# S5 rotation levels in wide operations, whole-table loads, an earlier SSD step-size stage and a split group norm, in a hybrid decoder trunk on one core

## The chip, the cores and the metric

One core of one Trainium2 chip runs the whole program. The core has a matrix engine (TensorE, "PE" in the profile; its weight loads are listed apart as "PEld"), three elementwise engines (VectorE "DVE", ScalarE "ACT", GpSimd "POOL") and a queue of DMA issues on SyncE ("SP"). Each engine takes its instructions in the order in which they stand on it, and semaphores make one engine wait for another. The metric is the time of the program on the device in microseconds; lower is better.

## The reference

Two decoder layers over 512 positions of width 1024, in float32. Layer 0 runs two sequence mixers side by side from one input projection, gates them, and projects back. Layer 1 is a multi-scale retention layer. Only layer 0 is touched here. Cut to what matters:

```python
def s5_mixer(u, ...):                  # 64 groups of 16 channels, 64 complex states each
    ab = exp(lr*dt) * (cos(li*dt) + 1j*sin(li*dt))      # one step of the state's decay and turn
    # x[t] = ab * x[t-1] + bb @ u[t]   (associative scan in chunks), y = Re(c @ x)
    y = gelu(y + d_skip*u)
    return y * sigmoid(y @ glu_w + glu_b)

def ssd_mixer(xbc, dt_raw, ...):       # 16 heads of 64, state 128
    xbc = silu(causal_depthwise_conv(xbc, conv_w, conv_b))
    dt = softplus(dt_raw + dt_bias)
    # chunked scan with decay exp(cumsum(-dt * exp(a_log)))

def rmsnorm(x, w, n_groups):           # SSD output times silu(z): two groups of 512 channels
    return x * rsqrt(mean(x*x, per group) + eps) * w
```

## The kernel before

Activations lie transposed: 128 channels on the partitions, 512 positions along the row, eight such tiles for the model width. A projection onto 128 output channels is a `proj`: in plain float32 (`mm1`, 8 matmuls of 512 columns), or for the names in `SPLIT` with weights and inputs split into a high and a low fp32r part (`mm3`, 24 matmuls). The accumulators of the projections (`acc`) are three PSUM tiles used in turn.

Layer 0 first normalises its input: squares on ACT, added on DVE, summed over the partitions on PE against a column of ones (`rs0ps`), inverse root on DVE (`rs0ms` to `rs0y`), spread over the partitions by transposes (`rs0pb`) and copied to `rbc`; `xn` is the product. Three S5 input projections, u0 to u2, run on the input that is not normalised yet, between the loads.

After that, layer 0 is a list of stages, `ORDER`. Each word is a letter and a number: x are the SSD input projections with their conv (DVE, three `scalar_tensor_tensor` on the PSUM tile), d the SSD step sizes (`steps`), e the decays (`decay`), u the S5 inputs, z the gates, q the S5 parameters, l and g the loading of an S5 block's input and tables, a its scan, k and b its taps, c its output, w the split of `xn`, s and t the SSD chunks, n and r the SSD norm, p the S5 gate, o the SSD half of the output projection. The list sets the priority; a scheduler then places each engine's instructions, so that the work of neighbouring stages is interleaved on an engine. The order on each engine is fixed when the program is built.

**The S5 rotation.** The scan needs a table `rot` with the turn of every state at every block of eight steps, 64 blocks for 32 columns of states. It is built by doubling, on POOL (`cmul`): from n blocks to 2n by a complex product with the turn at n blocks, the level `lv`. The levels come from DVE: `square()` squares a complex number of 32 columns and pulls its length back to one, ten small operations; it runs three times ahead of the first level and once between levels, and two copies write each level into `lvs`. All six levels cost 94 small DVE instructions.

**The tables.** `al_d` is a table in DRAM that the stage g reads back into `al` for each half block, `al[16 * tt:16 * tt + 16]` at a time, so that eight DMAs of 64 KB fill one `al`. The S5 input is written to `u_d` and read back to `U` in eight DMAs as well. The operators `T` of the taps are loaded in the same eight-piece manner.

**The products O.** Stage b forms the S5 output operators on POOL, `O<-ct,s5pws`, from a loaded table `ct`, eight products and four sums for each block.

**The SSD norm.** `ssd_norm` (stage n) loads a gate, applies it on POOL, squares on ACT into the gate's tile `zb`, and adds the squares of a group's four tiles on POOL. `ssd_parts` (stage r) calls `rstd`: four matmuls against ones (`rsg0ps`), the inverse root on DVE, the spread by transposes (`rsg0pb`), and then the products and splits into `ybh` and `ybl` that the output projection `ob` reads.

## Time and profile before

| | |
|---|---|
| time, median of 3 runs | 933.45 us (933.06 to 939.46) |
| the profiled execution, its own time | 927.74 us |
| its span in the profile | 925.9 us |
| busy: PE, DVE, ACT, POOL | 876.2, 553.2, 357.8, 226.2 us |
| instructions on PE, DVE, ACT, POOL | 4252, 986, 569, 193 |

The profiled execution took 927.74 us, of which the span covers 925.9; 1.8 us lie outside it. It was 5.7 us quicker than the median. Times in the profile are counted from the start of the span. Layer 0 takes its first 400 us and a little more.

### The profile page before, as it was taken

What the parts mean: (1) busy time and instruction counts of PE and PEld (TensorE: products, weight loads), DVE (VectorE), ACT (ScalarE), POOL (GpSimd) and SP (SyncE); (2) the same over time, 40 slices, a digit from 0 to 9 for tenths busy, and PEclk for the clock granted to TensorE, in tenths of its full rate; (3) what the DMA queues carried; (4) which work ended last, traced back from release to release, by engine and by line L of the source; (5) the groups of instructions that cost most, each with busy time, mean ns of one, the idle gap of its engine ahead of it and who ended that gap; (6) DMA issues with size and microseconds to landing.
All of it is one profiled execution on the core that took longest, in us unless ns stands there. A gap on an engine that the chain in (4) does not pass through costs nothing.

```text
span 925.9 us, 11510 instructions
## 1 busy us (share of the span) xinstructions
PE 876.2 (95%) x4252; PEld 670.6 (72%) x4252; DVE 553.2 (60%) x986; ACT 357.8 (39%) x569; POOL 226.2 (24%) x193
## 2 busy tenths in 40 slices
PE   8888898998989978999999999999999999999996
PEld 4323346776757766888888888888888888888885
DVE  7999847785893385733454464744643544547445
ACT  4312283252514453623433335345421243254442
POOL 0399445025380930000003121301000203110020
PEclk9998999997998988999999999999999999999999
...
GB/s 241 171 201 140 67 134 91 166 164 226 203 37 275 244 196 137 228 239 125 184 142 129 91 92 69 69 92 67 92 92 91 92 92 69 91 69 69 114 69 91
DMA packets 73623, 121.44 MB, mean 131 GB/s; under 512 B 27552, under 2 KB 38112, under 8 KB 73440
## 3 DMA queue, kind: packets, MB, share of 16 engines
...
q8 instruction: 33, 0.54, 0.2%
...
HBM read 103.61 MB, written 17.07 MB: 130 GB/s over the span
## 4 chain that ended last, share of the span: by engine, by line
PE 76%; DVE 7%; DMA 6%; ACT 4%; issue 3%; SPq 2%; POOL 2%; ACTq 0%; POOLq 0%
PE xbc L205 7%; PE g L115 3%; PE qk L117 3%; PE g L116 3%; PE qk L116 3%; PE g L117 3%; PE qk L115 3%; PE v L930 3%; PE v L931 3%; PE v L929 3%; PE z L117 2%; PE z L115 2%; PE z L116 2%; PE gl L115 2%; PE gl L116 2%
## 5 line engine op out<-in xcount | busy, mean ns | idle before, releaser
L903 POOL TENSOR_TENSOR rt<-rt,ru 128x512 f32<-128x512 f32 x16 | 27.2, 1721 | 134.7 <-DVE ru L902 134.7
L972 POOL TENSOR_TENSOR os<-os,os 128x512 f32<-128x512 f32 x12 | 15.5, 1292 | 139.8 <-ACT os L970 106.9
L798 POOL TENSOR_TENSOR O<-ct,s5pws 128x512 f32<-128x512 f32 x16 | 22.7, 1421 | 81.5 <-DMA ct<-in_s5c_dram 73.4
L882 POOL TENSOR_TENSOR hs<-hs,hs 128x512 f32<-128x512 f32 x7 | 12.3, 1757 | 92.4 <-ACT hs L880 92.4
L347 DVE SCALAR_TENSOR_TENSOR cva<-xbc,cvw,cva 128x511 f32<-128x511 f32 (+2 forms) x36 | 26.7, 741 | 12.3 <-ACT cva L344 11.9
L902 DVE TENSOR_TENSOR ru<-qk,tab 128x512 f32<-128x512 f32 x16 | 11.0, 686 | 32.4 <-PE qk L117 32.4
L392 ACT ACTIVATE dec<-dec,nacs 128x128 f32<-128x128 f32 x64 | 19.4, 389 | 16.6 <-DMA dec<-at_d 16.6
L349 ACT ACTIVATE cva<-cva 128x512 f32<-128x512 f32 x12 | 7.6, 630 | 41.3 <-DVE cva L347 41.2
L798 POOL TENSOR_TENSOR ot<-ct,s5pws 128x512 f32<-128x512 f32 x16 | 21.8, 1364 | 0.0
L802 POOL TENSOR_TENSOR O<-O,ot 128x512 f32<-128x512 f32 x16 | 21.6, 1379 | 0.0
L447 POOL TENSOR_TENSOR za6r<-za6r,y 128x512 f32<-128x512 f32 x1 | 2.0, 2044 | 79.2 <-ACT ob6h L107 79.2
L844 PE MATMUL Y<-Or,X 128*64 128x128 f32 x64 | 13.6, 297 | 8.1 <-DMA Or<-o_d 8.1
L1004 DVE TENSOR_TENSOR h<-h,out 128x512 f32<-128x512 f32 x8 | 5.5, 687 | 25.5 <-PE out L117 25.5
L1065 POOL TENSOR_TENSOR fin<-fin,fnw 128x512 f32<-128x512 f32 x4 | 5.0, 1294 | 58.5 <-ACT fq L1029 58.5
L516 DVE TENSOR_TENSOR h<-oa,h 128x512 f32<-128x512 f32 x8 | 5.5, 691 | 19.6 <-PE oa L117 19.6
L845 PE MATMUL Y<-T,U 128*64 128x128 f32 x128 | 16.7, 290 | 0.0
L411 PE MATMUL y<-ident,yos 128*128 128x128 f32 x48 | 12.7, 351 | 4.0 <-DVE yos L387 4.0
L487 DVE TENSOR_TENSOR hb<-ob,hb 128x512 f32<-128x512 f32 x8 | 5.5, 690 | 17.8 <-PE ob L117 17.8
L205 PE MATMUL xbc<-xn,xbc11w 128*128 128x512 f32 x16 | 9.2, 727 | 6.9 <-issue 6.9
L120 ACT ACTIVATE rh<-rt 128x512 fp32r<-128x512 f32 (+1 forms) x16 | 9.1, 577 | 16.9 <-POOL rt L903 16.9
L121 DVE TENSOR_TENSOR rl<-rt,rh 128x512 fp32r<-128x512 f32 (+1 forms) x16 | 14.9, 957 | 0.6 <-ACT rh L120 0.2
L411 PEld LDWEIGHTS y<-ident,yos 128*128 128x128 f32 x48 | 8.1, 209 | 9.2 <-issue 4.5
...
## 6 DMA issues: line engine op xcount, KB each, us to landing
al<-al_d SPq DMA_DIRECT2D x64, 64.0 KB, 3.3
...
b<-in_s5bP_dram SPq DMA_DIRECT2D x8, 512.0 KB, 4.5
dec<-at_d SPq DMA_DIRECT2D x8, 512.0 KB, 5.6
T<-kd SPq DMA_DIRECT2D x64, 64.0 KB, 2.7
...
```

What stands on the lines that cost most here:

```text
L115: pe.matmul(ps, wh[:, k, :], xh[k], start=start and i == 0, stop=False)
L116: pe.matmul(ps, wh[:, k, :], xl[k], start=False, stop=False)
L117: pe.matmul(ps, wl[:, k, :], xh[k], start=False, stop=stop and i == len(ks) - 1)
L205: pe.matmul(ps, raw[:, k, :], x[k], start=k == 0, stop=k == KD - 1)
L347: vec.scalar_tensor_tensor(g[:, d:], ps[:, 0:SEQ - d], cvw[:, m, j:j + 1], g[:, d:], op0=ALU.mult, op1=ALU.add)
L411: pe.matmul(ps_y[:, pr * P:(pr + 1) * P], yo[:, pr * P:(pr + 1) * P], ident, start=True, stop=False)
L798: pool.tensor_tensor(x.rearrange("p (g k c) -> p g k c", g=4, c=16), ct[:, c, par, 4 * hf:4 * hf + 4].unsqueeze(2).broadcast_to(sh), pws[: ...
L802: pool.tensor_tensor(o, o, tm, op=ALU.add)
L903: pool.tensor_tensor(t1, t1, t2, op=op)
L929: pe.matmul(ps[c], hh[kk][:, cs], wh[:, i, :], start=kk == 0, stop=False)
L930: pe.matmul(ps[c], hh[kk][:, cs], wl[:, i, :], start=False, stop=False)
L931: pe.matmul(ps[c], hl[kk][:, cs], wh[:, i, :], start=False, stop=kk == KD - 1)
```

## The change

The six levels of the rotation are no longer got by squaring one from the other. The angle of one block, `th`, is multiplied by 8, 16, ... 256 in six small operations into one tile of 192 columns, reduced to a turn, and put through the sine and cosine polynomial that the S5 parameters already use, now a function `sin_cos`. All levels are then there at once, after 25 DVE instructions of 192 or 384 columns in place of 94 of 32.

`al_d` has another layout, written by sixteen DMAs of eight partitions each, before two of 64; a whole `al` is then read by one DMA, and a whole `U` too. `T` keeps its eight pieces with another order of partitions.

In `ORDER` the step sizes d0 come first and the decays e0 right after x9. The input projection u2 leaves the head of the program (as 8 float32 matmuls) and stands beside u3 (as 24 split ones). r1 moves ahead of z10.

In the SSD norm the POOL additions go. PE sums the four square tiles of a group itself, sixteen matmuls against ones for each group in place of four; they and the inverse root (`root`) now belong to stage n, and the spread (`spread`) stays in stage r.

On DVE, just after the first normalisation, before. The names `s5scr` are the operands of `square()`; `cva` is a conv:

```order
L661 TENSOR_TENSOR s5scr_433<-s5scr_433 128x32
L662 TENSOR_TENSOR s5scr_433<-s5scr_433 128x32
L663 TENSOR_TENSOR s5scr_433<-s5scr_433 128x32
L347 SCALAR_TENSOR_TENSOR cva_268<-xbc_257,cvw,cva_268 128x511
L664 TENSOR_SCALAR s5scr_433<-s5scr_433 128x32
L347 SCALAR_TENSOR_TENSOR cva_268<-xbc_257,cvw,cva_268 128x510
L665 TENSOR_TENSOR s5scr_433<-s5scr_433 128x32
L666 TENSOR_TENSOR s5scr_433<-s5scr_433 128x32
L347 SCALAR_TENSOR_TENSOR cva_268<-xbc_257,cvw,cva_268 128x509
L675 COPY s5lv<-s5scr_433 128x32
L676 COPY s5lv<-s5scr_433 128x32
```

and after, at the place where the levels now begin; `s5al` is the table for `al_d`:

```order
L661 TENSOR_SCALAR s5lv_506<-s5scr_368 128x32 x6
L528 TENSOR_TENSOR s5cm_445<-s5pw,s5scr_436 128x8x32
L529 TENSOR_TENSOR s5cm_446<-s5pw,s5scr_436 128x8x32
L662 TENSOR_SCALAR s5lv_507<-s5lv_506 128x192
L530 TENSOR_TENSOR s5al<-s5cm_445,s5cm_446 128x8x32
L663 TENSOR_SCALAR s5lv_507<-s5lv_507 128x192
L665 SCALAR_TENSOR_TENSOR s5lv_506<-s5lv_507,s5lv_506 128x192 x3
L562 TENSOR_SCALAR s5lv_508<-s5lv_506 128x192
L563 SCALAR_TENSOR_TENSOR s5lv_507<-s5lv_508 128x192
L564 TENSOR_SCALAR s5lv_508<-s5lv_507 128x192
L352 SCALAR_TENSOR_TENSOR cva_293<-xbc_282,cvw,cva_293 128x511
```

The chain of small squarings that ran between the convs for all six levels has become one block of wider operations, which ends among the convs of xbc8 and xbc10; behind it no squaring stands on DVE.

On POOL, before, the end of the rotation and what follows it (`O` and `ot` are the second block's output operators):

```order
L522 TENSOR_TENSOR s5rt<-rot,s5lv 128x512
L523 TENSOR_TENSOR s5rt<-rot,s5lv 128x512
L524 TENSOR_TENSOR rot<-s5rt 128x32x16
L525 TENSOR_TENSOR s5rt<-rot,s5lv 128x512
L526 TENSOR_TENSOR s5rt<-rot,s5lv 128x512
L527 TENSOR_TENSOR rot<-s5rt 128x32x16
L798 TENSOR_TENSOR O_882<-ct_880,s5pws 128x512
L798 TENSOR_TENSOR ot_883<-ct_880,s5pws 128x512
L798 TENSOR_TENSOR O_888<-ct_880,s5pws 128x512
```

and after:

```order
L789 TENSOR_TENSOR O_808<-ct_794,s5pws 128x512
L789 TENSOR_TENSOR ot_809<-ct_794,s5pws 128x512
L789 TENSOR_TENSOR O_814<-ct_794,s5pws 128x512
L789 TENSOR_TENSOR ot_815<-ct_794,s5pws 128x512
L528 TENSOR_TENSOR s5rt<-rot,s5lv 128x512
L529 TENSOR_TENSOR s5rt<-rot,s5lv 128x512
L793 TENSOR_TENSOR O_796<-O_796,ot_797 128x512
L793 TENSOR_TENSOR O_802<-O_802,ot_803 128x512
L793 TENSOR_TENSOR O_808<-O_808,ot_809 128x512
L793 TENSOR_TENSOR O_814<-O_814,ot_815 128x512
L530 TENSOR_TENSOR rot<-s5rt 128x32x16
L733 TENSOR_TENSOR tm_958<-al_956,b_957 128x512 x2
```

The second block's products and sums stood behind the whole rotation; now they stand inside its last doubling, ahead of the last operation that completes `rot`.

On PE around the SSD norm, before; `K` are the S5 taps, `zb0r` and `zb4r` the tiles of squares, `ob` the output projection:

```order
L814 MATMUL K_2583<-O_1955,s5bd_651 32x128
L166 MATMUL rsg0ps<-ones,zb0r 128x1 x4
L172 MATMUL rsg0pb<-ident,rsg0y 128x128 x4
L166 MATMUL rsg1ps<-ones,zb4r 128x1 x4
L115 MATMUL ob_2889<-ybh_2636,ob0h 128x512
L115 MATMUL ob_2941<-ybh_2636,ob1h 128x512
L116 MATMUL ob_2889<-ybl_2637,ob0h 128x512
L117 MATMUL ob_2889<-ybh_2636,ob0l 128x512
L115 MATMUL ob_2889<-ybh_2641,ob0h 128x512
```

and after; z is the gate projection z9, `S` the scan input of the fourth S5 block:

```order
L115 MATMUL z_2581<-xh_913,z9h 128x512
L116 MATMUL z_2581<-xl_914,z9h 128x512
L166 MATMUL rsg0ps<-ones,zb0r 128x1
L166 MATMUL rsg0ps<-ones,zb1r 128x1
L746 MATMUL S_2268<-U_2121,tm_2125 64x64 x8
L166 MATMUL rsg0ps<-ones,zb2r 128x1
L746 MATMUL S_2268<-U_2121,tm_2136 64x64 x8
L117 MATMUL z_2581<-xh_913,z9l 128x512
```

The sum over the squares stood behind the taps and ahead of the output projection, one matmul for each 128 positions. Now it stands in the middle of the gate projection z9, one matmul for each of the four tiles (and each 128 positions), and each waits for its own tile.

```diff
@@ -26,15 +26,15 @@
 WARM = 11
-SPLIT = [f"z{m}" for m in range(16)] + [f"u{m}" for m in range(3, 8)]
+SPLIT = [f"z{m}" for m in range(16)] + [f"u{m}" for m in range(2, 8)]
 SILU_Z = tuple(range(8, 16))
 GELU_P = ()
 AX, AZ = 200, 600
 KEEP = (2, 3)
 POOL_Z = (7,)
 VEC_X = ((0, 0), (1, 0), (0, 1), (1, 1))
-ORDER = """x8 x10 d0 x9 x11 q0 x0 b0 x1 x2 l0 g0 x3 e0 x4 k0 x5 b1 x6 a0 x7 w0 g1 s0 u3 l1 t0 s1 z0 a1 k1 b2 z1 t1 s2 u4 c0 u5
- t2 l2 g2 s3 z2 a2 k2 b3 z3 t3 u6 c1 u7 z4 l3 g3 z5 n0 z6 a3 z7 c2 n1 z8 k3 r0 z9 z10 r1 c3 z11 o0 p0 p1 o1 z12 p2 z13 p3 o2 z14
+ORDER = """d0 x8 x10 x9 e0 x11 q0 x0 b0 x1 x2 l0 g0 x3 x4 k0 x5 b1 x6 a0 x7 w0 g1 s0 u2 u3 l1 t0 s1 z0 a1 k1 b2 z1 t1 s2 u4 c0 u5
+ t2 l2 g2 s3 z2 a2 k2 b3 z3 t3 u6 c1 u7 z4 l3 g3 z5 n0 z6 a3 z7 c2 n1 z8 k3 r0 z9 r1 z10 c3 z11 o0 p0 p1 o1 z12 p2 z13 p3 o2 z14
@@ -159,7 +159,7 @@
 
-    def rstd(sqs, n, name, bc):
+    def root(sqs, n, name):
@@ -167,10 +167,17 @@
         rsqrt_small(y, ps[:, 0:4], n, name)
+        return y
+
+    def spread(y, name, bc):
         pb = aux(name + "pb")
         for c in range(NC4):
             pe.transpose(pb[:, c * P:(c + 1) * P], y[:, c:c + 1].broadcast_to([P, P]), ident)
         act.activation(bc, pb, AF.Copy)
+
+    def rstd(sqs, n, name, bc):
+        y = root(sqs, n, name)
+        spread(y, name, bc)
...
@@ -235,12 +242,11 @@
                 sq.append(q)
-            pu = [acc(f"u{m}") if m < 2 else aux(f"u{m}", "b") for m in range(3)]
+            pu = [acc(f"u{m}") for m in range(2)]
             for k in range(KD):
                 pe.matmul(pu[0], w0[0][:, k, :], xs[k], start=k == 0, stop=k == KD - 1)
             rstd(sq[:1], D, "rs0", rbc)
             mm1(pu[1], w0[1], xs)
-            mm1(pu[2], w0[2], xs)
...
@@ -257,22 +263,21 @@
         def s5_in(m):
-            ps = proj(a["w_u"][m], f"u{m}") if m > 2 else pu[m]
+            ps = proj(a["w_u"][m], f"u{m}") if m > 1 else pu[m]
             with rank_e():
                 us = t("p", f"us{m}")
                 ud, sd = us.rearrange("p (t k) -> p t k", t=T5), ps.rearrange("p (k t) -> p t k", t=T5)
-                if m > 2:
+                if m > 1:
                     act.activation(ud, sd, AF.Copy)
                 else:
                     vec.tensor_tensor(ud, sd, rbc.rearrange("p (k t) -> p t k", t=T5), op=ALU.mult)
-                sp.dma_start(u_d[:, m * P:(m + 1) * P, :].rearrange("t c k -> c t k"),
-                             us.rearrange("p (t k) -> p t k", t=T5))
+                sp.dma_start(u_d[m * P:(m + 1) * P, :], us[:, 0:SEQ])
 
         def s5_begin(_):
             s5.update(s5_params(s5pr))
             s5_setup(s5)
 
-        for m in range(3):
+        for m in range(2):
@@ -459,15 +464,13 @@
                 act.activation(zt, yb[m], AF.Square)
-                if i:
-                    pool.tensor_tensor(sqs[0], sqs[0], zt, op=ALU.add)
                 sqs.append(zt)
-            held["sq", gr] = sqs
+            held["root", gr] = root(sqs, 512, f"rsg{gr}")
 
         def ssd_parts(gr):
-            yb, sqs = xbc[0:8], held["sq", gr]
+            yb = xbc[0:8]
             rg = t("m", f"rg{gr}")
-            rstd(sqs[:1], 512, f"rsg{gr}", rg)
+            spread(held["root", gr], f"rsg{gr}", rg)
@@ -555,6 +558,17 @@
 
+        def sin_cos(hh, qq, zz, th, n):
+            vec.tensor_scalar(hh[:, 0], th, 0.5, None, op0=ALU.mult)
+            vec.scalar_tensor_tensor(n, hh[:, 0], -1.0, hh[:, 0], op0=ALU.mult, op1=ALU.max)
+            vec.tensor_scalar(hh[:, 1], n, -1.0, 0.5 * math.pi, op0=ALU.mult, op1=ALU.add)
+            vec.tensor_tensor(zz, hh, hh, op=ALU.mult)
+            vec.tensor_scalar(qq, zz, 1.0 / math.factorial(13), None, op0=ALU.mult)
+            for k in (11, 9, 7, 5, 3):
+                sg = 1.0 if (k // 2) % 2 == 0 else -1.0
+                vec.scalar_tensor_tensor(qq, qq, sg / math.factorial(k), zz, op0=ALU.add, op1=ALU.mult)
+            vec.scalar_tensor_tensor(qq, qq, 1.0, hh, op0=ALU.add, op1=ALU.mult)
+
@@ -575,19 +589,9 @@
             vec.scalar_tensor_tensor(th, n, -cst, th, op0=ALU.mult, op1=ALU.add)
-        hh = scr2[:, 0]
-        vec.tensor_scalar(hh[:, 0:W], th, 0.5, None, op0=ALU.mult)
-        vec.scalar_tensor_tensor(n, hh[:, 0:W], -1.0, hh[:, 0:W], op0=ALU.mult, op1=ALU.max)
-        vec.tensor_scalar(hh[:, W:], n, -1.0, 0.5 * math.pi, op0=ALU.mult, op1=ALU.add)
-        zz = scr2[:, 1]
-        vec.tensor_tensor(zz, hh, hh, op=ALU.mult)
-        qq = scr2[:, 2]
-        vec.tensor_scalar(qq, zz, 1.0 / math.factorial(13), None, op0=ALU.mult)
-        for k in (11, 9, 7, 5, 3):
-            sg = 1.0 if (k // 2) % 2 == 0 else -1.0
-            vec.scalar_tensor_tensor(qq, qq, sg / math.factorial(k), zz, op0=ALU.add, op1=ALU.mult)
-        vec.scalar_tensor_tensor(qq, qq, 1.0, hh, op0=ALU.add, op1=ALU.mult)
-        sh, ch = qq[:, 0:W], qq[:, W:]
+        hh, zz, qq = (scr2[:, i].rearrange("p (i w) -> p i w", w=W) for i in range(3))
+        sin_cos(hh, qq, zz, th, n)
+        sh, ch = qq[:, 0], qq[:, 1]
@@ -636,10 +640,11 @@
                 act.activation(pws[64:128, par, 1:8, c], pw[q, 0:7, c, 0:32], AF.Copy, scale=1.0 - 2.0 * c)
-        al_d = dp.tile([8, 2, 64, 2, 32], F32, name="al_d")
-        for h in range(2):
-            sp.dma_start(al_d[:, :, :, h].rearrange("k c x f -> x (k c) f"),
-                         al[64 * h:64 * h + 64].rearrange("p k c f -> p (k c) f"))
+        al_d = dp.tile([8, T5, 2, 8, 2, 32], F32, name="al_d")
+        for jp in range(8):
+            for h in range(2):
+                sp.dma_start(al_d[jp, :, :, :, h].rearrange("k c x f -> x (k c) f"),
+                             al[64 * h + 8 * jp:64 * h + 8 * jp + 8].rearrange("p k c f -> p (k c) f"))
@@ -647,33 +652,26 @@
         pool.memset(rot[:, 1, :, 0:1], 0.0)
-        h32 = [P, 32]
-        scr4 = scr4[:, 0:192].rearrange("p (i w) -> p i w", w=32)
-        ca, sa, cb_, sb_, w1, w2 = (scr4[:, i] for i in range(6))
-        vec.tensor_scalar(ca, cm_[:, 0:32], 1.0, None, op0=ALU.add)
-        vec.tensor_copy(sa, st[:, 0:32])
-
-        def square():
-            vec.tensor_tensor(w1, ca, ca, op=ALU.mult)
-            vec.tensor_tensor(w2, sa, sa, op=ALU.mult)
-            vec.scalar_tensor_tensor(sb_, ca, 2.0, sa, op0=ALU.mult, op1=ALU.mult)
-            vec.tensor_tensor(cb_, w1, w2, op=ALU.subtract)
-            vec.tensor_tensor(w1, cb_, cb_, op=ALU.mult)
-            vec.tensor_tensor(w2, sb_, sb_, op=ALU.mult)
-            vec.tensor_tensor(w1, w1, w2, op=ALU.add)
-            vec.tensor_scalar(w1, w1, -0.5, 1.5, op0=ALU.mult, op1=ALU.add)
-            vec.tensor_tensor(ca, cb_, w1, op=ALU.mult)
-            vec.tensor_tensor(sa, sb_, w1, op=ALU.mult)
-
-        for _ in range(3):
-            square()
+        lvs = t("m", "s5lv", n=384).rearrange("p (n i w) -> p n i w", i=2, w=32)
+        NL = 6
+        sl = [P, NL, 32]
+        ang, cnt_, sc, q2 = (f(f"s5lv{i}", [P, 2, NL, 32]) for i in range(4))
+        th_, n_ = ang[:, 0], cnt_[:, 0]
+        for i in range(NL):
+            vec.tensor_scalar(th_[:, i], th[:, 0:32], 8.0 * 2 ** i, None, op0=ALU.mult)
+        vec.tensor_scalar(n_, th_, 0.5 / math.pi, MAGIC, op0=ALU.mult, op1=ALU.add)
+        vec.tensor_scalar(n_, n_, MAGIC, None, op0=ALU.subtract)
+        for cst in (TWO_PI_1, TWO_PI_2, TWO_PI_3):
+            vec.scalar_tensor_tensor(th_, n_, -cst, th_, op0=ALU.mult, op1=ALU.add)
+        sin_cos(sc, q2, cnt_, th_, n_)
+        sh, ch = q2[:, 0], q2[:, 1]
+        vec.scalar_tensor_tensor(lvs[:, :, 1], sh, 2.0, ch, op0=ALU.mult, op1=ALU.mult)
+        vec.scalar_tensor_tensor(n_, sh, -2.0, sh, op0=ALU.mult, op1=ALU.mult)
+        vec.tensor_scalar(lvs[:, :, 0], n_, 1.0, None, op0=ALU.add)
         n = 1
         rt = f("s5rt", [P, 2, 32, 16])
-        lvs = t("m", "s5lv", n=384).rearrange("p (n i w) -> p n i w", i=2, w=32)
         while n < NK:
             lv = lvs[:, n.bit_length() - 1]
-            vec.tensor_copy(lv[:, 0], ca)
-            vec.tensor_copy(lv[:, 1], sa)
@@ -682,8 +680,6 @@
             n *= 2
-            if n < NK:
-                square()
@@ -722,20 +718,15 @@
         U = f(f"U{j}", [P, 16, NK])
-        for tt in range(T5):
-            sp.dma_start(U[16 * tt:16 * tt + 16],
-                         u_d[tt, 256 * j:256 * j + 256, :].rearrange("(g c) k -> c g k", c=16))
+        sp.dma_start(U, u_d[256 * j:256 * j + 256, :].rearrange("(g c) (t k) -> (c t) g k", c=16, k=NK))
         s5["U"][j] = U
 
     def s5_state(s5, j):
         s5["P"][j] = []
         for par in range(2):
-            g0 = 16 * j + 8 * par
             al, b, tm = (f(f"{n}{j}{par}", [P, 2, 8, 2, 32]) for n in ("al", "b", "tm"))
-            for tt in range(T5):
-                src = s5["al_d"][T5 - 1 - tt, :, g0:g0 + 8].rearrange("c g h f -> c (g h f)")
-                sp.dma_start(al[16 * tt:16 * tt + 16].rearrange("p c g h f -> p c (g h f)"),
-                             src.partition_broadcast(16))
+            src = s5["al_d"][2 * j + par].rearrange("k c g h f -> k (c g h f)")[::-1]
+            sp.dma_start(al.rearrange("p c g h f -> p (c g h f)"), src.unsqueeze(0).broadcast_to([16, T5, 1024]))
...
```

## Rows read from the trace of the kernel before

**Rows 1.** The page: busy time, share and instructions by engine.
```profile
PE 876.2 (95%) x4252; PEld 670.6 (72%) x4252; DVE 553.2 (60%) x986; ACT 357.8 (39%) x569; POOL 226.2 (24%) x193
```

**Rows 2.** Windows: busy time (instructions) of PE, PEld, DVE, ACT, POOL; PEclk, DMA.
```profile
60.00:80.00 20.00, 13.11 (x29) 5.44 (x28) 19.59 (x42) 3.05 (x4) 19.01 (x28) 0.83 0.57 163
...
400.00:925.00 525.00, 517.41 (x2419) 433.16 (x2417) 263.55 (x427) 196.69 (x294) 62.05 (x40) 1.00 0.30 100
```

**Rows 3.** PE, in order of time; start, duration, [idle before <-releaser].
```profile
24.41 0.95 PE L166 MATMUL rs0ps<-ones,xq 128*128 128x1 f32 x8
...
35.37 8.82 PE L205 MATMUL xbc<-xn,xbc8w 128*128 128x512 f32 x16 [1.62 <-DVE xn L245]
44.02 7.03 PE L205 MATMUL xbc<-xn,xbc10w 128*128 128x512 f32 x16
...
71.98 3.75 PE L205 MATMUL xbc<-xn,xbc11w 128*128 128x512 f32 x4 [6.89 <-issue]
...
99.52 8.80 PE L205 MATMUL xbc<-xn,xbc2w 128*128 128x512 f32 x16 [4.12 <-issue]
```

**Rows 4.** DVE, groups in the first 125 us, mean ns of one.
```profile
L663 DVE TENSOR_TENSOR s5scr<-s5scr 128x32 f32<-128x32 f32 x8 | 4.1, 509 | 0.1
...
L675 DVE COPY s5lv<-s5scr 128x32 f32<-128x32 f32 x6 | 1.8, 295 | 0.0
```

**Rows 5.** DVE, in order of time, around the first normalisation.
```profile
25.39 0.16 DVE L150 TENSOR_SCALAR rs0ms<-rs0ps 128x4 f32<-128x4 f32 x1
...
32.81 0.17 DVE L159 SCALAR_TENSOR_TENSOR rs0y<-rs0t,rs0y 128x4 f32<-128x4 f32 x1
...
33.91 0.19 DVE L661 TENSOR_TENSOR s5scr<-s5scr 128x32 f32<-128x32 f32 x1
...
34.63 5.14 DVE L245 TENSOR_TENSOR xn<-x,rbc 128x512 f32<-128x512 f32 x8
...
47.55 1.14 DVE L661 TENSOR_TENSOR s5scr<-s5scr 128x32 f32<-128x32 f32 x1
```

**Rows 6.** POOL, in order of time.
```profile
33.46 0.27 POOL L522 TENSOR_TENSOR s5rt<-rot,s5lv 128x32 f32<-128x32 f32 x1 [31.87 <-DVE s5lv L676]
...
41.21 0.62 POOL L711 TENSOR_TENSOR s5cm<-s5scr,s5bA 128x256 f32<-128x256 f32 x1 [3.90 <-DMA s5bA<-in_s5bA_dram]
...
102.25 1.27 POOL L527 TENSOR_TENSOR rot<-s5rt 128x512 f32<-128x512 f32 x1
129.18 1.10 POOL L798 TENSOR_TENSOR O<-ct,s5pws 128x512 f32<-128x512 f32 x1 [25.66 <-DMA ct<-in_s5c_dram]
...
137.66 4.94 POOL L802 TENSOR_TENSOR O<-O,ot 128x512 f32<-128x512 f32 x4
```

**Rows 7.** DVE, in order of time, first scan to the split of z1.
```profile
146.53 0.67 DVE L767 TENSOR_TENSOR gi<-S,rot 128x504 f32<-128x504 f32 x1
...
167.37 1.22 DVE L108 TENSOR_TENSOR z1l<-z1w,z1h 128x1024 fp32r<-128x1024 f32 x1
```

**Rows 8.** PE, in order of time, where z1 begins.
```profile
168.83 0.39 PE L115 MATMUL z<-xh,z1h 128*128 128x512 f32 x1
169.06 0.40 PE L116 MATMUL z<-xl,z1h 128*128 128x512 f32 x1
```

**Rows 9.** PE, in order of time, z9 and the SSD norm.
```profile
313.34 0.50 PE L117 MATMUL z<-xh,z9l 128*128 128x512 f32 x1 [1.33 <-DVE z9l L108]
...
345.04 1.09 PE L172 MATMUL rsg0pb<-ident,rsg0y 128*128 128x128 f32 x4 [4.65 <-DVE rsg0y L159]
...
361.10 0.40 PE L844 MATMUL Y<-Or,X 128*64 128x128 f32 x2 [2.30 <-DMA Or<-o_d]
```

**Rows 10.** POOL, in order of time, the SSD norm.
```profile
312.16 2.26 POOL L460 TENSOR_TENSOR cva<-cva,zb3r 128x512 f32<-128x512 f32 x1
```

**Rows 11.** The page: DMA issues, count, KB each, us to landing.
```profile
al<-al_d SPq DMA_DIRECT2D x64, 64.0 KB, 3.3
...
b<-in_s5bP_dram SPq DMA_DIRECT2D x8, 512.0 KB, 4.5
```

More of the change, by code (lines that the diff above doesn't have):

```diff
@@ L229, in layer0 @@
                     w0 += [ld_raw(a["w_u"][m], f"u{m}") for m in range(1)]
-            w0 += [ld_raw(a["w_u"][m], f"u{m}") for m in range(1, 3)]
+            w0 += [ld_raw(a["w_u"][m], f"u{m}") for m in range(1, 2)]
             for k in range(KD):
@@ L250, in layer0 @@
         s5 = {}
-        u_d = dp.tile([T5, D, NK], F32, name="u_d")
+        u_d = dp.tile([D, T5 * NK], F32, name="u_d")
         def parts(_):
@@ L834, in s5_out @@
                 src = kd[j, :, hf, P - 16 * tt:2 * P - 16 * tt].rearrange("(q c) l -> c q l", c=16)
-                sp.dma_start(x[16 * tt:16 * tt + 16], src)
+                sp.dma_start(x[tt::T5], src)
             Tp.append(x)
@@ L1108, in _layout @@
     bp = b.reshape(2, 4, 2, 8, 2, 32, 16).transpose(1, 2, 6, 0, 3, 4, 5)
-    r["s5bP"] = np.broadcast_to(bp[:, :, None], (4, 2, 8, 16, 2, 8, 2, 32)).reshape(4, 2, P, 2, 8, 2, 32)
+    r["s5bP"] = np.broadcast_to(bp[:, :, :, None], (4, 2, 16, 8, 2, 8, 2, 32)).reshape(4, 2, P, 2, 8, 2, 32)
     r["eye"] = np.tile(np.eye(16, dtype=np.float32), (8, 1))
```

## The prediction, made before the changed kernel ran

> **What bounds the kernel now.** The page comes first. PE is busy 876.2 of 925.9 us [rows 1], so what is not matmul is under 50 us. Then the windows, to see where it lies: from 400 us on PE is busy 517.41 of 525 [rows 2], which leaves 7.6 us in more than half of the program. Nothing of the change touches that part, and nothing is to be had there. What idles is layer 0: 49.7 − 7.6, some 42 us before 400. In one stretch there, 60 to 80, PE is busy 13.11 of 20 us, with a granted clock of 0.83, while DVE is busy 19.59 and POOL 19.01 [rows 2]: there the two elementwise engines set the pace.
>
> The timeline of PE shows why. The SSD input projections follow each other at 7.03 us, with two gaps, 6.89 us ahead of xbc11 and 4.12 us ahead of xbc2 [rows 3]. Both are marked "issue": the accumulators go round in three, and the conv on DVE that frees the next one was late. DVE was late because of the squarings. In the first 125 us they make twelve groups of lines, from 4.1 us (mean 509 ns) down to 1.8 us (mean 295 ns) [rows 4]; I summed the twelve to 34.4 us. One alone takes 0.19 us, the same line 1.14 us once POOL works beside it [rows 5], and POOL's products there take 1.10 us each [rows 6]: a small DVE operation waits out a POOL instruction.
>
> The third place is z1. The first scan's `gi` waits for the whole table `rot`. From there DVE works down a list, 146.53 to the split `z1l` at 167.37, which takes 1.22 [rows 7], and z1 starts on PE at 168.83 [rows 8], right behind it. So between layer 0's SSD projections and z1 it is DVE's list that sets PE's time, and what sets the start of that list is part of the question. The fourth place is the SSD norm: PE idles 4.65 us for the inverse root, and 2.30 us for a load behind it [rows 9].
>
> **The start.** Ahead of `rs0ps` PE had 18 of the 24 early float32 matmuls in its order; now 12 of 16 stand there. A matmul costs 7.03 / 8 = 0.88 us [rows 3], so `rs0ps` comes up to 5.3 us earlier than 24.41 [rows 3]: 19.1, and I take 19.5, since the sum of squares on DVE must be there too. From the first to the last of the root's operations DVE took 25.39 to 32.98, 7.6 us [rows 5], because some thirty squarings and copies stood between; they leave, at a step of 0.1 us each, and about a third of the gain goes back to parameter work that slides in. I take 5.5. `xn`, at 34.63 before [rows 5], then begins near 27, 7.6 us earlier. Bounds: 5 and 9.
>
> **The SSD projections.** After `xn` PE has d0 first (8.8 us, as the first eight matmuls took at 35.37 [rows 3]), then twelve projections at 7.03 = 84.4, and 7 us of small work of d, e and s (estimate). That ends at 27.7 + 8.8 + 84.4 + 7.1 = 128, if the two gaps of 6.89 and 4.12 don't come back. DVE has about 2.2 us of conv for each 7 us of PE, and no squarings. The vectorised levels are 25 operations on up to 384 columns, at most some 17 us by the 0.67 us of a 504-column one [rows 7], and rather 9 by their width. They end among the convs of xbc8 and xbc10, so the conv of xbc10 bounds them: PE ends it near 51, and the last level is there at 54 to 55. So the two gaps go, 11 us, on the way. Bound for what returns of them: 0 to 4 us.
>
> **The rotation on POOL.** This is the counterweight. POOL began it at 33.46, as soon as the first level was there, and ended at 102.25 + 1.27 = 103.5; 70 us, of which 3.90 were a wait for a load [rows 6]. Now the first level comes with the last, at 54 to 55, some 21 us later. Besides, the second block's products (129.18 to 142.6, 13.4 us [rows 6]) now stand inside the last doubling, ahead of the operation that completes `rot`. So: 55 + 3 (the table s5bA, now behind sixteen small writes on SP; estimate) + 66.1 (its work without that wait) + 13.4 = 137.5. In the first 70 us many products were stretched by DVE's small operations, as DVE's by them. I take 7 to 8 off for that, so `rot` is whole near 130. Bounds 126 (all stretched products at 1.10 to 1.27 us [rows 6]) and 138 (nothing off). Before, `rot` was whole at 103.5 and not last for the scan.
>
> From `gi` to the end of `z1l` DVE took 168.6 − 146.5 = 22 us [rows 7]. In the new order 6.5 us more stand between them (u3's split at 1.2, four products of the tables at 0.67 or more, and some that moved). So z1 starts at 129.5 + 28.5 = 158, against 168.83 [rows 8]: **11 us earlier**. u2's 24 split matmuls, 24 × 0.23 = 5.5 us (the step of 168.83 to 169.06 [rows 8]), lie ahead of z1 and are inside that. Bounds: 2 us (rot at 138) and 22 (rot not last, PE's own list decides).
>
> Here the Trainium skill has a rule, in "SBUF — State Buffer", section "Who interferes with whom": a DVE operation with two SBUF inputs and a GpSimd instruction that reads SBUF exclude each other for the whole instruction, whoever came first. The 0.19 us that became 1.14 beside products of 1.10 [rows 5, 6] agree. By it POOL gains as well when DVE's hundred small operations go; the sum takes this as 7 to 8 us, from the rows.
>
> **The DMAs.** 56 issues of `al` and 28 of `U` leave SP, 14 for `al_d` come. A 64 KB piece lands 3.3 us after its issue, a 512 KB load 4.5 [rows 11]; eight pieces in a row land a little later than one whole load. None of them ended a wait of PE that is counted above. I take 0, bounds −2 to +2. The Trainium skill, "DMA: Bandwidth & Descriptors", section "Rules for kernel authors", speaks against the writes: an outermost dimension of under 16 keeps a DMA to that many engines, and the `al_d` writes have eight partitions. No row shows such a write, and by that rule they would land later by a few us, ahead of loads that the scan does not wait for last.
>
> **The SSD norm.** 24 more matmuls against ones at some 0.24 us (eight rows in 0.95 us [rows 3], two rows to a matmul): +5.7 us on PE, at a stage where PE is the bound. Lower bound +4.8. In return the 4.65 us ahead of `rsg0pb` go, as the root lies under z9 and z10; of the 2.30 us ahead of Y perhaps all [rows 9]. But the taps no longer cover the split into `ybh`, and I leave 2 us of idle: −5. Net +0.7, taken as 0; bounds −3 and +4.
>
> **Sum.** −11 (start, gaps and rotation together) + 0 + 0 = −11. Against the profiled execution, 927.74, that is 916.7; against the median, 933.45, it is **922**. With the terms' bounds: −22 − 3 = −25 and −2 + 4 = +2.
>
> **The rivals.** *A, the forecast:* POOL's rotation decides z1; 922. Chance 0.42.
>
> *B, POOL is not last.* Undisturbed, POOL could end `rot` by 119, if the products never stretch and s5bA is early; then PE's and DVE's own lists set z1, at about 147. −22 − 2: 909. For it speaks that POOL's products in the second half of the rotation already ran at 1.27 [rows 6]. Against it, the convs and splits that now run beside it. Chance 0.26.
>
> *C, POOL is last by more.* If `rot` is whole only at 140.4 (168.83 − 28.5), nothing of the front is left: the time is 931 to 934. For it speaks that the contention is mutual and that DVE's work now is wider. Chance 0.20. That the wide levels don't free DVE, because each waits out POOL, hardly can be: POOL has nothing to do until the levels are there (31.87 us of idle before 33.46 [rows 6]).
>
> *D, slower.* The matmuls on the squares stand in z9, in PE's fixed order, and wait for POOL's products with the gates. One of those took 2.26 us at 312.16 [rows 10], others 1.28. In the new order the last two products of the S5 tables, and the loads that they wait for, stand ahead of them on POOL. z9's third matmul stood at 313.34 [rows 9]; 11 us earlier, and with the fourth block's scan sums (2.8 us, estimate) and 13 matmuls of 0.23 ahead, PE comes to the last tile's matmul near 308. The square comes near 301: 312.16 + 2.26, less the two POOL sums of 1.3 that stood ahead, less 11. If the tables' load is late, PE stands still with z9 half done, and z10 and all the rest queue behind it. The gain of 11 is used up at a stall of 11 us; at 20 us the kernel is slower by 1%. Seven products at 1.28 us from a load that lands at 312 give a stall of 14, 936; at 2.26 us and a load at 315 it is 24, 946. I take 944. Chance 0.08. Something else that gives no change: 0.04.
>
> **How the numbers follow.** The likeliest is A, 922. A measurement of this kernel can tell about 1%, 9.3 us, from no change. Faster by more: B, and some two thirds of A: 0.54. Slower by more: D, and a part of C with a rotation later than 145: 0.12. The rest, 0.34. The range takes in B, with the norm at its lower bound of −3, and C: 906 to 934, which leaves out D and the tails.
>
> **What the changed profile would show.** `xn` on DVE near 27 in place of 34.63; PE without the gaps of 6.89 and 4.12; POOL's first rotation product near 55, the last near 130; `gi` right behind it and z1 near 158; `rsg0ps` inside z9 with no idle time ahead of it, and no 4.65 us ahead of `rsg0pb`. If `gi` starts well after the last rotation product, B holds; if z1 starts at 168 or later, C; if PE idles inside z9 with POOL or ACT as releaser, D. What would upset all of it is a new wait on an accumulator or a tile buffer in the SSD projections, which the order does not show.

## The result and the profile after

The changed kernel took 923.73 us (median of 7 runs, 920.36 to 925.25), the kernel before 933.45 (7 runs, 927.67 to 939.46). The ratio is 0.9885 with a 95% interval of 0.9848 to 0.9923: faster by 1.2%, 9.7 us, where 11 were forecast. The profiled execution took 923.73 us, the median; that of before was one of its quickest. So the two spans lie only 4.0 us apart, and stages are compared here by differences within a profile, which can shift by some 2 us from one execution to the next (the arrival of the first loads alone moved `rs0ps` between 19.2 and 21.7 in kernels with the same start). The 9.7 us are a difference of medians; what the two traces can account for is 4.0.

First the page and the windows (busy time of PE, PEld, DVE, ACT and POOL with instructions, granted clock, DMA share, GB/s):

```profile
span 921.9 us, 11425 instructions
...
PE 881.6 (96%) x4308; PEld 678.6 (74%) x4308; DVE 524.6 (57%) x917; ACT 360.3 (39%) x571; POOL 212.7 (23%) x187
```

```profile
60.00:80.00 20.00, 20.00 (x56) 9.17 (x54) 15.42 (x19) 3.05 (x4) 19.63 (x20) 1.00 0.71 202
80.00:100.00 20.00, 14.47 (x35) 6.14 (x34) 8.82 (x12) 17.80 (x35) 19.00 (x28) 0.99 0.69 247
...
300.00:320.00 20.00, 18.37 (x130) 16.31 (x129) 6.15 (x14) 7.32 (x12) 11.44 (x10) 0.83 0.67 209
...
400.00:921.00 521.00, 513.39 (x2401) 429.96 (x2399) 262.54 (x426) 195.50 (x292) 62.18 (x40) 1.00 0.30 100
```

Beside [rows 1, 2]: from 400 on nothing changed, 7.6 us idle in both. PE is full from 60 to 80, where it had 13.11 us. But from 80 to 100 it has only 14.47, while DVE is busy 8.82 and ACT 17.80: another engine is late there now. PE is 5.4 us busier in all.

PE in order of time, against [rows 3, 8]:

```profile
19.33 0.95 PE L166 MATMUL rs0ps<-ones,xq 128*128 128x1 f32 x8
...
81.27 7.11 PE L212 MATMUL xbc<-xn,xbc2w 128*128 128x512 f32 x16 [1.11 <-issue]
...
100.64 9.93 PE L212 MATMUL xbc<-xn,xbc4w 128*128 128x512 f32 x16 [5.06 <-issue]
...
129.17 7.13 PE L212 MATMUL xbc<-xn,xbc7w 128*128 128x512 f32 x16
...
157.16 0.50 PE L115 MATMUL z<-xh,z1h 128*128 128x512 f32 x1 [0.62 <-ACT z1h L107]
```

The start came as forecast, z1 too. Between them two gaps came back, at xbc2 and xbc4. ACT shows whose they are:

```profile
76.08 0.36 ACT L334 ACTIVATE dcd<-dcd 128x192 f32<-128x192 f32 x1 [9.10 <-DVE dcd L332]
81.25 1.28 ACT L354 ACT_TABLE_LOAD   x1 [4.81 <-DVE cva L352]
...
83.08 0.76 ACT L349 ACTIVATE cva<-xbc,cvw 128x512 f32<-128x512 f32 x1
83.74 4.77 ACT L397 ACTIVATE dec<-dec,nacs 128x128 f32<-128x128 f32 x16
88.53 1.28 ACT L398 ACT_TABLE_LOAD   x1
...
92.72 2.43 ACT L397 ACTIVATE dec<-dec,nacs 128x128 f32<-128x128 f32 x8
...
97.42 0.76 ACT L349 ACTIVATE cva<-xbc,cvw 128x512 f32<-128x512 f32 x1
```

L349 is the copy out of the accumulator with which each conv begins. Between two of them, from 83.84 to 97.42, ACT computes mostly the first chunks' decay tables (`dec`) and changes its function tables at 1.28 us each; of the 17.80 us that it is busy from 80 to 100, four such changes are 5.1. The decays come that early because d0 and e0 do. The accumulators were waiting again, now for ACT. The copy at 83.08 was late as well: ACT had idled 9.10 us for `dcd` and 4.81 for a conv ahead of it, both from DVE. xbc4, behind the second gap, took 9.93 us in place of 7.03, at a granted clock of 0.84 from 100 to 120.

DVE at the start, and around the first scan, against [rows 5, 7]:

```profile
27.29 4.90 DVE L251 TENSOR_TENSOR xn<-x,rbc 128x512 f32<-128x512 f32 x8
```

```profile
126.39 0.75 DVE L352 SCALAR_TENSOR_TENSOR cva<-xbc,cvw,cva 128x511 f32<-128x511 f32 x1 [4.55 <-ACT cva L349]
127.06 3.31 DVE L733 TENSOR_TENSOR tm<-al,b 128x512 f32<-128x512 f32 x2
130.29 0.73 DVE L352 SCALAR_TENSOR_TENSOR cva<-xbc,cvw,cva 128x510 f32<-128x510 f32 x1
130.95 0.67 DVE L758 TENSOR_TENSOR gi<-S,rot 128x504 f32<-128x504 f32 x1
...
136.27 0.67 DVE L759 TENSOR_TENSOR X<-S,rot 128x504 f32<-128x504 f32 x1
```

and POOL's rotation, against [rows 6]:

```profile
54.40 0.27 POOL L526 TENSOR_TENSOR s5rt<-rot,s5lv 128x32 f32<-128x32 f32 x1 [52.81 <-DVE s5lv L668]
...
113.91 1.28 POOL L527 TENSOR_TENSOR rot<-s5rt 128x512 f32<-128x512 f32 x1
...
131.45 1.28 POOL L530 TENSOR_TENSOR rot<-s5rt 128x512 f32<-128x512 f32 x1
```

The rotation begins and ends where it was expected. But the first `gi` starts at 130.95, before the last rotation product ends at 132.73, and DVE does not wait for POOL there. By the kernel's code `gi` reads only the cosine half of `rot`, whole at 115.19 (113.91 + 1.28); the sine half, which the last product writes, is first read by `X` at 136.27, 3.5 us after it is whole. DVE's last wait was 4.55 us for the conv of xbc6, which PE ended at 125.54. In the kernel before the same `gi` at 146.53 stood behind the conv of the same xbc6, too. ACT's copies of xbc6, before and after:

```profile
145.07 0.76 ACT L344 ACTIVATE cva<-xbc,cvw 128x512 f32<-128x512 f32 x1
```

```profile
125.58 0.78 ACT L349 ACTIVATE cva<-xbc,cvw 128x512 f32<-128x512 f32 x1 [3.01 <-PE xbc L212]
```

Before, PE had ended xbc6 at 138.60 and ACT copied it 6.5 us later; now it copies at once.

Last, PE at the SSD norm, against [rows 9]:

```profile
305.89 0.38 PE L166 MATMUL rsg0ps<-ones,zb2r 128*128 128x1 f32 x2 [1.63 <-ACT zb2r L466]
...
345.82 0.80 PE L115 MATMUL ob<-ybh,ob0h 128*128 128x512 f32 x1 [2.20 <-ACT ybh L120]
```

The 4.65 us are gone, but a wait of 1.63 has come inside z9, with a granted clock of 0.83 in that window, and 2.20 ahead of `ob`. By the first matmul of z8, PE was 9.16 us ahead of before (296.79 for 305.95), and at the first of ob3 3.95 (395.44 for 399.39). The stage between took 98.65 us where it had taken 93.44: 5.2 us of the gain were given back. The 3.95 that are left are the 4.0 between the two spans.

### The profile page after: what moved, and what is told of

It reads as the page before. It is cut to its first block, busy times and chain, and to the rows that moved or that the text cites. A ratio compares the mean times of both kernels' runs of the same rounds, so it can differ in the third digit from the quotient of the medians.

```text
span 921.9 us, 11425 instructions
## 1 busy us (share of the span) xinstructions
PE 881.6 (96%) x4308; PEld 678.6 (74%) x4308; DVE 524.6 (57%) x917; ACT 360.3 (39%) x571; POOL 212.7 (23%) x187
## 4 chain that ended last, share of the span: by engine, by line
PE 76%; DVE 11%; issue 4%; ACT 4%; DMA 2%; POOL 1%; SPq 0%; DVEq 0%; POOLq 0%; ACTq 0%
PE xbc L212 3%; PE qk L117 3%; PE g L115 3%; PE qk L116 3%; PE g L116 3%; PE g L117 3%; PE qk L115 3%; PE v L921 3%; PE v L922 3%; PE v L920 3%; PE z L117 2%; PE z L115 2%; PE z L116 2%; PE ob L116 2%; PE ob L117 2%
## 5 line engine op out<-in xcount | busy, mean ns | idle before, releaser
L793 POOL TENSOR_TENSOR O<-O,ot 128x512 f32<-128x512 f32 x16 | 24.6, 1563 | 0.0
L789 POOL TENSOR_TENSOR ot<-ct,s5pws 128x512 f32<-128x512 f32 x16 | 21.7, 1355 | 0.0
L733 POOL TENSOR_TENSOR tm<-al,b 128x512 f32<-128x512 f32 x6 | 8.1, 1371 | 55.6 <-DMA b<-in_s5bP_dram 32.9
L526 POOL TENSOR_TENSOR s5rt<-rot,s5lv 128x512 f32<-128x512 f32 (+4 forms) x7 | 5.9, 837 | 52.8 <-DVE s5lv L668 52.8
L839 ACT ACTIVATE ysb<-Y 128x256 f32<-128x256 f32 x16 | 5.2, 380 | 29.9 <-PE Y L836 18.8
L733 DVE TENSOR_TENSOR tm<-al,b 128x512 f32<-128x512 f32 x10 | 11.3, 1168 | 9.9 <-DMA b<-in_s5bP_dram 6.8
```

The lines of the kernel that those rows point to most:

```text
L789: pool.tensor_tensor(x.rearrange("p (g k c) -> p g k c", g=4, c=16), ct[:, c, par, 4 * hf:4 * hf + 4].unsqueeze(2).broadcast_to(sh), pws[: ...
L793: pool.tensor_tensor(o, o, tm, op=ALU.add)
```

## The experiments

All ratios are to the kernel before, measured beside it. Its median there was 929.14, 931.85 or 933.26 us, so results of different groups are compared by their ratios, and a ratio times 933.45 is set against the forecasts. One trace was kept of each kernel. Each of the first four makes one part of the change alone.

**Levels alone.**

```diff
-            vec.tensor_copy(lv[:, 0], ca)
-            vec.tensor_copy(lv[:, 1], sa)
-            if n < NK:
-                square()
+        sin_cos(sc, q2, cnt_, th_, n_)
...
```

> The kernel before with the wide rotation levels alone (nothing else of the change). My theory: the squarings on DVE were what held up the SSD projections, so the gaps of 6.89 and 4.12 us on PE go and z1 comes earlier by 5 to 11 us although POOL begins the rotation some 20 us later; the time is 924 to 929 where the kernel before has 933.5. Rival: POOL, begun 20 us later, is last for the first scan, z1 stays near 168 and the time is 931 to 935.

Measured: 921.28 us, ratio 0.9909 (0.9889 to 0.993). xbc7 ends at 140.51 (before 149.35), z1 begins at 159.34, z8 at 298.44. Of the gaps one of 3.63 us is left. My theory held, in time too (0.9909 of 933.45 is 925): this part alone makes most of the gain of the whole change.

**Order alone.**

```diff
-SPLIT = [f"z{m}" for m in range(16)] + [f"u{m}" for m in range(3, 8)]
+SPLIT = [f"z{m}" for m in range(16)] + [f"u{m}" for m in range(2, 8)]
...
-ORDER = """x8 x10 d0 x9 x11 q0 x0 b0 x1 x2 l0 g0 x3 e0 x4 k0 x5 b1 x6 a0 x7 w0 g1 s0 u3 l1
+ORDER = """d0 x8 x10 x9 e0 x11 q0 x0 b0 x1 x2 l0 g0 x3 x4 k0 x5 b1 x6 a0 x7 w0 g1 s0 u2 u3 l1
...
```

> The kernel before with the other stage order alone (step sizes first, decays after x9, u2 beside u3, r1 before z10). My theory: xn comes 5 us earlier, but the squarings still hold up the convs, so most of it is lost again at the gaps; the time is 929 to 934. Rival: the order is what brings the whole gain, 922 to 926.

Measured: 936.12 us, ratio 1.0084 (1.0061 to 1.0107); slower, beyond both expectations. PE and DVE in that kernel:

```profile
75.54 0.66 PE L321 MATMUL ps_a<-dda,tri 128*128 128x64 f32 x2 [10.31 <-issue]
```

```profile
74.61 0.70 DVE L663 TENSOR_SCALAR s5scr<-s5scr 128x32 f32<-128x32 f32 x1
75.23 0.21 DVE L313 SCALAR_TENSOR_TENSOR dda<-dtn,ea 128x64 f32<-128x64 f32 x1
```

The decays' matmul now stands among the early projections in PE's order, and waits 10.31 us for the last of the step sizes, `dda`, whose chain of small operations alternates on DVE with the squarings (`s5scr`). In the changed kernel, with the wide levels, the same `dda` is there at 58.96 and PE does not wait. The parts are not additive: this wait needs the squarings beside it. The order loses beside the levels too, as levels and order shows below.

**Norm alone.**

```diff
-                if i:
-                    pool.tensor_tensor(sqs[0], sqs[0], zt, op=ALU.add)
-            held["sq", gr] = sqs
+            held["root", gr] = root(sqs, 512, f"rsg{gr}")
...
-            rstd(sqs[:1], 512, f"rsg{gr}", rg)
+            spread(held["root", gr], f"rsg{gr}", rg)
```

> The kernel before with the split SSD norm alone (squares summed on PE, root in the earlier stage). My theory, from the profile of the changed kernel: 24 more matmuls with one column cost 5 to 6 us on PE, and the clock granted to PE is lower around them, while some 5 us of waits go; the time is 933 to 938. Rival: the wait of 4.65 us for the root is what counts, 928 to 931.

Measured: 938.58 us, ratio 1.0105 (1.0076 to 1.0135). The stage from z8 to ob3 takes 105.0 us where it had 93.4. The rival falls, and the loss is larger than my theory gave (1.0105 of 933.45 is 943).

**Layouts alone.**

```diff
-        al_d = dp.tile([8, 2, 64, 2, 32], F32, name="al_d")
+        al_d = dp.tile([8, T5, 2, 8, 2, 32], F32, name="al_d")
-        u_d = dp.tile([T5, D, NK], F32, name="u_d")
+        u_d = dp.tile([D, T5 * NK], F32, name="u_d")
-                sp.dma_start(x[16 * tt:16 * tt + 16], src)
+                sp.dma_start(x[tt::T5], src)
...
```

> The kernel before with the new table and input layouts alone (sixteen writes of the table, one load per table and per input block, pieces of T in another order of partitions). My theory: none of these transfers ends a wait of PE in the first 170 us, and one issue in place of eight brings a load ahead of its queue a little later on; 931 to 935. Rival: the shorter SP queue brings the Or loads forward (8.1 us of PE waits before), 926 to 929.

Measured: 934.45 us, ratio 1.0043 (1.0021 to 1.0064): a slight loss, a little beyond my theory (by the ratio 937), and no gain from the shorter queue: the waits for `Or` add up to 9.4 us. The stage from z8 to ob3 takes 98.7 us here, 5.3 more than before, though the norm is as it was.

**The squares back on POOL** in the changed kernel:

```diff
+                if i:
+                    pool.tensor_tensor(sqs[0], sqs[0], zt, op=ALU.add)
                 sqs.append(zt)
-            held["root", gr] = root(sqs, 512, f"rsg{gr}")
+            held["root", gr] = root(sqs[:1], 512, f"rsg{gr}")
```

> The changed kernel with the squares of the SSD norm summed on POOL again (root and spread stay apart, four matmuls against ones in place of sixteen for each group). My theory: the matmuls against ones and the lower clock around them are what loses 5 us between z8 and ob3; ob3 comes 3 to 6 us earlier after z8 and the time is 917 to 921 where the changed kernel has 923.7. Rival: the new place of the root and of r1 and the order of the loads lose it; the time stays 922 to 926.

Measured: 922.31 us, ratio 0.9893 (0.9859 to 0.9928). The stage is shorter, as expected (z8 to ob3 94.90 for 98.65), but the time is not to be told from the changed kernel's, as the rival had it. In this profile z8 came 3.7 us later, of which 2.4 are the first loads (`rs0ps` at 21.71 for 19.33).

**The decays late** in the changed kernel:

```diff
-d0 x8 x10 x9 e0 x11 q0 x0 b0 x1 x2 l0 g0 x3 x4
+d0 x8 x10 x9 x11 q0 x0 b0 x1 x2 l0 g0 x3 e0 x4
```

> The changed kernel with the decays e0 back behind x3 (the step sizes d0 stay first). My theory: the gaps of 1.11 and 5.06 us on PE at xbc2 and xbc4 come from ACT, which computes the first chunk's decay tables ahead of the convs' copies; they go, the SSD projections end 6 to 9 us earlier, but POOL ends the rotation at 131 to 133 as now and becomes the one that is waited for, so z1 moves by 0 to 3 us; 920 to 924. Rival: ACT alone was the bound and z1 comes 7 to 9 us earlier; 914 to 917.

Measured: 930.62 us, ratio 0.9985 (0.9956 to 1.0014): the gain is gone, which neither theory gave. The two gaps went and xbc7 ended 9.1 us earlier (127.22), so the early decays were needed for the gaps; that they are not enough, levels and order shows below. z1 came at 157.81, and POOL was waited for, both as my theory had it, but the wait is not at `gi`:

```profile
125.80 1.28 POOL L530 TENSOR_TENSOR rot<-s5rt 128x512 f32<-128x512 f32 x1
```

```profile
127.12 3.44 DVE L733 TENSOR_TENSOR tm<-al,b 128x512 f32<-128x512 f32 x2 [4.74 <-POOL rot L530]
```

```profile
139.77 0.80 PE L116 MATMUL u<-xl,u2h 128*128 128x512 f32 x1 [8.46 <-DVE xl L121]
```

Ahead of `gi` DVE works the products `tm` of the next tables, released by the rotation's last product, and runs them stretched beside POOL (3.44 us for two, which take 1.29 in the next kernel, where POOL is idle); behind `gi` stand the splits `xl` that PE's u2 waits 8.46 us for. Here the Trainium skill's rule of "SBUF — State Buffer", section "Who interferes with whom" (a DVE operation with two SBUF inputs and a reading GpSimd instruction exclude each other), fits these rows. The lead of 9 us became that wait. z8 came at 302.69, 5.9 us later than in the changed kernel; what was lost between z1 and z8 is not settled.

**The second block's products late** in the changed kernel:

```diff
-x5 b1 x6 a0 x7 w0 g1 s0
+x5 x6 a0 x7 w0 g1 b1 s0
```

> The changed kernel with the second block's products O (b1) in a later place, so that the rotation table on POOL is whole before them. My theory: the table is whole near 119 in place of 132.7, but DVE comes to the scan only behind the conv of xbc6, which PE ends at 125.5, so z1 moves by 0 to 3 us; 920 to 924. Rival, as the prediction had it: the rotation is what the scan waits for, and z1 comes 8 to 11 us earlier; 913 to 916.

Measured: 935.06 us, ratio 1.0025 (1.0001 to 1.0049). The rotation was whole at 121.6 in place of 132.7, and `gi` started at 130.14, 0.8 us earlier than in the changed kernel:

```profile
130.14 0.67 DVE L758 TENSOR_TENSOR gi<-S,rot 128x504 f32<-128x504 f32 x1
```

The rival's 8 to 11 us did not come. But this run does not free the scan from the rotation, for DVE idles for its last product here too, ahead of `tm`, and the conv of xbc5 stands behind `tm`:

```profile
121.59 1.29 DVE L733 TENSOR_TENSOR tm<-al,b 128x512 f32<-128x512 f32 x2 [6.88 <-POOL rot L530]
```

```profile
127.36 0.63 ACT L354 ACTIVATE cva<-cva 128x512 f32<-128x512 f32 x1 [10.43 <-DVE cva L352]
```

From 121.59 DVE works without idle time up to the end of that conv; ACT waits for it, copies xbc6 right behind, and `gi` follows. So the rotation is at the head of the chain to `gi` in this kernel, by way of `tm`. In the changed kernel `tm` started at 127.06, ahead of the rotation's last product. That the time would stay was wrong too: the products moved into the scan's own stretch, and z8 came at 311.99, 15 us later than in the changed kernel.

**Both late**, the two edits above together.

> The changed kernel with both moves: decays behind x3 and the second block's products behind the rotation. My theory: the two limits on the first scan (ACT, which delays the convs, and POOL, which ends the rotation) lie within a few us of each other, so only both together bring z1 forward, by 5 to 9 us; 914 to 919. Rival: a third limit right behind them (the loads of the tables for the second block, PE's own list) holds z1 where it is; 920 to 924.

Measured: 935.79 us, ratio 1.0043 (1.0017 to 1.0069). `gi` at 130.11, z8 at 312.47. Neither time came. The scan stayed where it was, as the rival had it, but not by a third limit: DVE idles 7.08 us for the rotation's last product ahead of `tm`, and the convs and `gi` stand behind it, as in the kernel above.

**The norm as before** in the changed kernel (the norm's pieces undone), with r1 ahead of z10 and then behind it:

```diff
-r0 z9 r1 z10
+r0 z9 z10 r1
```

> The changed kernel with the whole SSD norm as before (squares added on POOL, root and spread together in stage r); levels, order and layouts stay. My theory: the part of the norm costs in the full change what the stage from z8 to ob3 lost, 4 to 6 us; the time is 917 to 920 where the changed kernel has 923.7. Rival: with the squares back on POOL alone the time hardly moved (922.3), so the split norm is neutral in the full change; 921 to 925.

> The changed kernel with the whole SSD norm as before and r1 back behind z10. My theory: r1 in its former place gives the root's wait the same cover as before, ob3 comes 1 to 2 us earlier than with r1 ahead of z10; 916 to 919. Rival: the earlier r1 was worth having; 921 to 925.

Measured: 923.16 us, ratio 0.9901 (0.9873 to 0.9929), and 923.65, 0.9907 (0.9881 to 0.9933). Both misses: the stage from z8 to ob3 takes 94.6 us in both, 4 less than in the changed kernel, and the time does not move. z8 came 2.2 and 4.9 us later in these profiles. So in the full change the split norm is neutral, the rival's reading.

**Levels and order**: the edits of levels alone and order alone together, but r1 behind z10; no layouts, norm as before.

> The kernel before with the wide levels, the step sizes first, the decays after x9 and u2 beside u3; no new layouts, the norm and r1 as before. My theory: the order lost 8 us alone because the chain of step sizes ran among the squarings and PE waited 10.31 us for it; with the levels that chain is short, so the order now gains, z1 near 157 in place of 159.3 with the levels alone; 916 to 920. Rival: the order is a loss in any company (ACT's decay tables ahead of the convs); 923 to 928.

Measured: 929.63 us, ratio 0.9968 (0.9945 to 0.9991). xbc7 ended at 126.19, 23 us ahead of the kernel before, z1 began at 155.80, 13 ahead, z8 at 302.29, 3.7 ahead. The lead at xbc7 is not kept: of the 10 us lost up to z1, some 5.5 (24 × 0.23, an estimate) are u2's split matmuls, which now stand there, and PE waits for the splits `xl` again:

```profile
137.50 0.80 PE L116 MATMUL u<-xl,u2h 128*128 128x512 f32 x1 [5.62 <-DVE xl L121]
```

My theory falls, the rival's number is close, but not its reason: no gap ahead of the convs is in this profile, though the decays are as early and ACT is as busy (16.81 of 20 us from 80 to 100). A copy stands between its decay tables:

```profile
87.19 0.76 ACT L343 ACTIVATE cva<-xbc,cvw 128x512 f32<-128x512 f32 x1
```

With the layouts beside levels and order (the norm as before, r1 ahead of z10), the gaps are there, 1.10 and 5.05 us. So early decays alone don't make them; the place of each copy in the order on ACT and DVE does, and the layouts shift it too.

**Levels and layouts**: the edits of levels alone and layouts alone together.

> The kernel before with the wide levels and the new table and input layouts; order and norm as before. My theory: the layouts move loads by a few us in either direction and are worth nothing on their own, 921 to 926 where the levels alone have 921.3. Rival: with DVE free the loads become what is waited for, and the shorter queue gains; 916 to 920.

Measured: 918.83 us, ratio 0.9864 (0.9831 to 0.9896), the lowest of all. The rival's number was right. In the kernel with the levels alone PE waited 5.63 us for the second block's `Or`, with the layouts 1.09; from z1 to z8 it took 134.0 us in place of 139.1. But behind z8 the wait for the fourth block's grew from 3.39 to 5.11, and from z8 to ob3 it took 99.8 us in place of 95.8. First the levels alone, then with the layouts:

```profile
272.01 0.66 PE L836 MATMUL Y<-Or,X 128*64 128x128 f32 x2 [5.63 <-DMA Or<-o_d]
...
354.00 0.40 PE L836 MATMUL Y<-Or,X 128*64 128x128 f32 x2 [3.39 <-DMA Or<-o_d]
```

```profile
266.07 0.40 PE L831 MATMUL Y<-Or,X 128*64 128x128 f32 x2 [1.09 <-DMA Or<-o_d]
...
350.49 0.66 PE L831 MATMUL Y<-Or,X 128*64 128x128 f32 x2 [5.11 <-DMA Or<-o_d]
```

Over the whole of layer 0 the waits for `Or` are no shorter with the layouts (10.5 us for 9.3), so the rival's reason, loads that gain, is not shown.

## Why the prediction was right, and where not

**The start: right.** `rs0ps` at 19.33 (19.5 forecast), the root from 20.32 to 25.51, 5.2 us (5.5), `xn` at 27.29 (27; the prediction's own terms, 4.9 and 2.1 us earlier, give 27.6). What it is worth is another matter: with the levels alone `xn` stays late, and the time differs from the changed kernel's by less than the intervals.

**The gaps: the mechanism right, the end of it wrong.** DVE's squarings were what delayed the convs; take them away alone and the gain is 0.9%. But xbc7 ended at 136.3, not 128. I looked for what comes late next on DVE only; a new wait on an accumulator was named as what would upset it, without a price. The step sizes and decays that moved forward put ACT's decay work ahead of the convs' copies: 6.2 us of gaps, and xbc4 at 9.93 in place of 7.03, against a bound of 4. Decays late shows that they were needed, as the gaps leave with them; in levels and order the same early decays make no gap, so the order on ACT and DVE that came with the layouts is part of the cause. A part of ACT's time there is table changes; the Trainium skill, "ScalarE: Activation LUTs", section "What ACT_TABLE_LOAD costs", gives about 1283 ns for one, and the rows have 1.28 us.

**The rotation on POOL: timed right, its role wrong.** First product at 54.40 (54 to 55), whole at 132.7 (130). The step "`rot` decides the scan" failed in the changed kernel: `gi`, which it had wait for the whole table, began 1.8 us before the rotation was whole, and the half that came last was read 3.5 us after. What decided was the conv of xbc6 in DVE's order, and thus PE's own projections and ACT's delay, before as after. PE ended xbc6 13.1 us earlier than before, and ACT's 6.5 us of delay behind it went; DVE's two products `tm`, 3.31 us, came in between. That z1 came at 157.16 for 158 is therefore luck, a right number from the wrong limit; two limits lay within 2 us of each other. How much the rotation would have held with the other limit gone is open: in the three kernels with a part moved late, DVE waits 4.74 to 7.08 us for it ahead of `tm`, and `gi` comes no earlier than 130.1. By its condition this is rival B, POOL not last, but without B's z1 at 147. And `z1l` was misread as what z1 starts behind: before, the first matmul of z1 came without idle time [rows 8] and does not read `z1l`; after, it waits 0.62 us for the high part from ACT, and the split of `z1l` begins only at 161.12. By the split the gain is 6.3 us, not 11.7. By z8 it is 9.2.

**The norm: mis-sized.** Net 0 was taken, −3 to +4; the stage cost 5.2 us. The matmuls' price was right (+5.7 forecast; PE is busy 8.69 us with `rsg0ps` and `rsg1ps`, before 2.76); what was missing is the wait of 1.63 us for the squares and a lower granted clock (0.83 from 300 to 320, before 1.00; 0.70 from 340 to 360, before 0.66), whose price no run isolates. Alone this part costs 1.05%. In the full change its removal shortens the stage by 4 us and gives nothing measurable in time; where those 4 us go again is not settled. Nor is the stage's length the norm's alone: kernels with the norm as before took 95.8 (levels), 98.7 (layouts), 99.0 (levels and order) and 99.8 us (levels and layouts) for it. Rival D's mechanism was there, at 1.63 us and not 20.

**The layouts: 0 taken, with the right sign for neither company.** Alone they lose 0.4%, beside the levels they gain some 0.45% (0.9864 for 0.9909; the intervals overlap a little), some 4 us either way, where the bounds were −2 and +2. Beside levels and order they gain 0.6% (0.9907 for 0.9968). One wait for `Or` became shorter and a later one longer, so why they gain stays open. The sixteen writes of the table hold SP's issues from 41.0 to 48.7 us, where two had taken 32.9 to 34.3. I had searched for waits only ahead of z1.

**The sum.** −11 forecast, −9.7 measured. That the two lie so close is luck in part: the −11 were all at z1, the traces have 9.2 us left by z8 and 4.0 at the end, and the rest of the 9.7 is that the profiled execution of the kernel before ran 5.7 us under its median, which no trace explains. The sum of the bounds left out the layouts' −2 and +2; with them it is −27 and +4. By parts it was made otherwise: levels −0.9%, layouts some −0.45%, order a loss (beside the levels it changes 0.9909 into 0.9968; with levels and layouts, norm as before, 0.9864 into 0.9907, where the intervals overlap), norm about nothing in full company. What the order loses in company was seen only as a lead that shrinks from 23 us at xbc7 to 13 at z1 and 3.7 at z8.
